# Prompt attention kept feature-major: probabilities divided by their sums ahead of their transposes, mean of squares by one matmul

## Chip, cores and metric

One core of one Trainium2 chip. The time is that of the device for one execution, in microseconds (us), as the median of several runs. The engines are named as in the profile: PE (matrix multiplications and transposes; PEld is its weight load), DVE (elementwise work), ACT (activations and copies), POOL (elementwise work, slower), SP (issues most DMAs). PE writes to PSUM, eight banks of 128 x 512 f32; all other tiles lie in SBUF.

## What is computed

One inference step of a decoder layer for a prompt of 1024 tokens and 8 running sequences ("samples") of 8 tokens each, width 1024, all in float32. What matters here is the middle of the layer, the mixer:

```
z = rms_norm(x) @ w_in + b_in          # q, k, v of attention; four parts of a linear recurrence (HGRN2)
# sliding window attention, 8 heads of 64 in 2 groups, window 128, one sink per head
p = exp(s - m);  den = sum(p) + exp(sink - m);  a = (p / den) @ v
a = rms_norm(a) * attn_out_norm        # mean of squares over all 512 features of a token
mix = concat([a, gated recurrence]) @ w_out
x = x + rms_norm(mix) * norm_mix_post
```

In front of it and behind it stands a gated FFN of width 2816 each (w_gu, w_down), which makes up most of the multiplications.

## The kernel before

**Tiling.** The 1088 tokens are worked in three groups of 320, 384 and 384 (`WIDTH`); group 0 holds 256 prompt tokens and the 64 sample tokens. Attention runs in blocks of 128 prompt tokens, two, three and three of them (`NPB`), so eight in all. Each large product is made of three PE instructions on operands split into a rounded part and a remainder (`mm3`, L260 to L262); `split` (L240, L241) makes the parts, a copy on ACT and a subtraction on DVE. Weights stream in through `raw` tiles, are split, and are used once.

**Order.** The mixer of a group is a Python generator (`mixer`, L1635): it joins the chain of recurrence steps with the chain of attention blocks and yields between pieces of work. `tick()` advances it a little after each half of a streamed product (`stream`, `tick`, L99 to L110), so that the mixer's small PE instructions lie between the large products of `w_in_units`, `w_out_units` and the FFNs; `need` runs the rest of it at once. The program is then put in order at build time from a simulated timeline (`schedule_with_timeline_sim=True`, L1921): on each engine the earliest piece of program whose inputs are ready by that simulation goes first. At run time every engine works through its queue in that order.

**An attention block** (`attn_block`, L1215) works on pairs of heads, `pr` = 0 and 1, in both groups of heads at once. The scores `sc` (L1237) go through a masked maximum on DVE (L1247) and an exponential on ACT (L1255) with the queries as rows; the exponential's sum goes to `mx[:, 1]`, and L1259 makes the sink's exponential. Two yields later PE transposes the probabilities (`pT`, L1269), ACT and DVE copy them to SBUF (L1274), and one yield later the products `pv` (L1283) with the values give the result feature-major: the feature as the row, the query as the column, in `of_`. After the second pair, the sums and the sink are added and inverted for all heads (L1296, L1297), and PE transposes `of_` back to queries as rows (`pvT`, L1301, four instructions); DVE multiplies by the inverted sums as it evicts (L1303).

`finish_attn` (L1199) then normalizes: a square with its sum on ACT (L1202), an inverse root on one column on DVE (L1203 and `rsqrt`, L224 to L229), a multiplication with the root and the gain `aon` (L1205). Three yields later PE transposes the result once more (`oT`, L1211, four instructions), and `put_mix` (L1193) splits it into `MT`, the input of `w_out`: a copy on ACT (L1196), the remainder on DVE (L1197). The samples have an attention of their own (`sample_attn`, L1470), with queries as rows throughout, which ends in the same `finish_attn`. `w_out_units(0)` takes all 320 tokens of group 0 in each product, so it waits for the samples too.

**Buffers.** Small tiles come from `t2` (8 buffers in SBUF) and `ax` (4 PSUM banks), shared by all streams. `mean_root` (L290) is the inverse root for the other norms: one matmul with a constant matrix sums over the rows, and six DVE and two ACT instructions follow.

Of the kernel before, what the change touches and what calls it, by code (L numbers as in the profile page):

```python
# [47 lines left out]
def tile_step(ctx: ExitStack, tc: tile.TileContext, A: dict, O: list):  # L48
# [17 lines left out]
    def axbank(s="ax"):  # L66
        return ps.tile([P, 512], F32, tag="ax", bufs=4, name=uid(s))
# [219 lines left out]
    def tmp2(name, shape=(P, 512)):  # L287
        return pp.tile(list(shape), F32, tag="t2", bufs=8, name=uid(name))

    def mean_root(ss, dst=None):  # L290
        w = ss.shape[-1]
        bank = axbank("rb")
        y = tmp2("rt")[:, :w]
        x = bank[:, :w]
        made = PE.matmul(x, omean, ss, start=True, stop=True)
        t = tmp2("mt")[:, :w]
        V.tensor_scalar(y.bitcast(I32), x.bitcast(I32), -0.5, float(MAGIC), op0=ALU.mult, op1=ALU.add)
        S.activation(t, y, AF.Square)
        V.tensor_tensor(t, x, t, op=ALU.mult)
        V.scalar_tensor_tensor(y, t, -3.0 * RS ** 2, y, op0=ALU.add, op1=ALU.mult)  # L300
        S.activation(t, y, AF.Square)
        V.tensor_tensor(t, x, t, op=ALU.mult)
        q = tmp2("mq")[:, :w]
        V.scalar_tensor_tensor(q, t, -40.0 / 3 * RS ** 6, t, op0=ALU.add, op1=ALU.mult)
        end = V.scalar_tensor_tensor(x if dst is None else dst, q, 80.0 * RS ** 12, y, op0=ALU.add, op1=ALU.mult)
        return made, x, end

    def sum_squares(E, ss, sq, d):
# [770 lines left out]
    def mixing(tp, h):  # L1079
        w_in, w_out = A["w_in"], A["w_out"][0]  # L1080

        def t2(shape=(P, 512)):
            return tmp2("t2", shape)

        aon = tp.tile([P, 512], F32, tag="aon", name="aon")
        nc.sync.dma_start(aon, A["attn_out_norm"][0:1].partition_broadcast(P))
        bhi = tp.tile([P, 512], F32, tag="bhi", name="bhi")
        nc.sync.dma_start(bhi, A["b_in"][0:1, 1792:2304].partition_broadcast(P))

# [103 lines left out]
        def put_mix(n, half, sl, src):  # L1193

            hi, lo = MT[n][0][half], MT[n][1][half]
            S.copy(hi[:, :, sl], src)  # L1196
            V.tensor_tensor(lo[:, :, sl], src, hi[:, :, sl].bitcast(F32), op=ALU.subtract)  # L1197

        def finish_attn(n, o, r, sl):  # L1199

            sm = small()
            S.activation(junk[:r], o[:r], AF.Square, accum_out=sm[:r, 0, 0:1])  # L1202
            V.tensor_scalar(sm[:r, 0, 0:1], sm[:r, 0, 0:1], 1.0 / 512, EPS, op0=ALU.mult, op1=ALU.add)  # L1203
            rsqrt(sm[:r, 1, 0:1], sm[:r, 0, 0:1], (sm[:r, 2, 0:1], sm[:r, 3, 0:1]))
            V.scalar_tensor_tensor(o[:r], o[:r], sm[:r, 1, 0:1], aon[:r], op0=ALU.mult, op1=ALU.mult)  # L1205
            yield
            yield
            yield
            b4 = axbank("oT").rearrange("p (c t) -> p c t", c=4)
            for c in range(4):  # L1210
                PE.transpose(b4[:, c, :r], o[:r, c * P:(c + 1) * P], ident[:r, :r])  # L1211
            put_mix(n, 0, sl, b4[:, :, :r])
            yield

        def attn_block(n, b):  # L1215
# [9 lines left out]
            def of(x, pr):  # L1225
                return x.rearrange("p (g r i) -> p g r i", g=2, r=2)[:, :, pr]
# [4 lines left out]
            for pr in range(2):  # L1231
# [25 lines left out]
                                     scale=0.125, accum_out=mx[:, 1, hd:hd + 1])  # L1257
                V.tensor_tensor(of(sm[:, 2], pr), of(sm[:, 1], pr), of(nsinkb, pr), op=ALU.subtract)
                S.activation(of(sm[:, 2], pr), of(sm[:, 2], pr), AF.Exp)  # L1259
                yield  # L1260
                yield
                pT, tb2 = [], [axbank("pT").rearrange("p (g i s q) -> p g i s q", g=2, i=2, s=2) for _ in range(2)]
# [28 lines left out]
                else:  # L1291
                    S.copy(src, ob[0])
                    V.tensor_tensor(src, ob[1], src, op=ALU.add)
                if pr:
                    yield
            V.tensor_tensor(mx[:, 2], mx[:, 1], sm[:, 2], op=ALU.add)  # L1296
            V.reciprocal(mx[:, 3], mx[:, 2])  # L1297
            yield
            tb = axbank("pvT")
            for m in range(4):  # L1300
                PE.transpose(tb[:, m * P:(m + 1) * P], of_[:, m * P:(m + 1) * P], ident)  # L1301
            o = t2()
            V.tensor_tensor(o.rearrange("p (g m d) -> p m g d", g=2, m=4),  # L1303
                            tb.rearrange("p (m g d) -> p m g d", m=4, g=2),
                            mx[:, 3].rearrange("p (g m) -> p m g", g=2).unsqueeze(3).to_broadcast([P, 4, 2, 64]),
                            op=ALU.mult)
            yield from finish_attn(n, o, P, slice(b * P, (b + 1) * P))

        def intra(n, res):

# [159 lines left out]
        def sample_attn():  # L1470
# [65 lines left out]
            for b in range(8):  # L1536
                for g in range(2):
                    nc.sync.dma_start(
                        o[8 * b:8 * b + 8, 256 * g:256 * g + 256].rearrange("t (m d) -> t m d", m=4),
                        osc[2 * g + b // 4, 32 * (b % 4):32 * (b % 4) + 32].rearrange("(m t) d -> t m d", m=4))  # L1540
            yield
            yield from finish_attn(n, o, NS, slice(256, 320))
# [318 lines left out]
def _laid_out(inputs):  # L1861

    import numpy as np

    a = {k: np.asarray(v) for k, v in inputs.items()}

    def columns(x):
        return x.reshape(-1, P).T

    def feature_major(x):  # L1870
        return x.T.reshape(KC, P, -1).transpose(1, 0, 2).reshape(P, -1)

# [6 lines left out]
    out = {k: a[k] for k in ("cache_k_win", "cache_v_win", "state_hgrn", "b_in", "attn_sinks", "attn_out_norm", "w_out",  # L1879
                             "ffn1_w_down",  # L1880
                             "ffn2_w_down", "norm_ffn1_post", "norm_mix_post", "norm_ffn2_post")}
    out.update(
        x0T=feature_major(np.concatenate([xp[:256], a["x_sample"].reshape(NS, D)])),
        xT=np.stack([feature_major(xp[256:640]), feature_major(xp[640:1024])]),
        x_rest=xp[256:],
        ffn1_w_gu=tiles(a["ffn1_w_gu"][0]), ffn2_w_gu=tiles(a["ffn2_w_gu"][0]), w_in=tiles(w_in[:, paired]),
        w_val=w_in[:, 1792:2304].reshape(4, 2, P, 512).transpose(0, 2, 1, 3).reshape(4, P, 1024),
        norm_ffn1_pre=columns(a["norm_ffn1_pre"]),
        cols=np.concatenate([columns(x) for x in (
            a["norm_ffn1_post"], a["norm_mix_pre"], a["norm_mix_post"], a["norm_ffn2_pre"], a["norm_ffn2_post"],  # L1890
            b[paired], a["hg_lb_logits"], a["hg_out_norm"], a["attn_out_norm"])], axis=1),
        sample_sinks=np.tile(np.repeat(a["attn_sinks"].reshape(2, 4).T, 8, axis=0), (4, 1)),
        cache_kT=a["cache_k_win"][0].reshape(8, P, P).transpose(2, 0, 1).reshape(P, 8 * P))
    return {k: np.ascontiguousarray(v) for k, v in out.items()}
# [30 lines left out]
```

## Time and profile before

| | |
|---|---|
| median of 3 runs | 1935.81 us (1934.51 to 1936.41) |
| the profiled execution | 1934.69 us, span of its instructions 1933.0 us |
| granted PE clock | 0.999 |
| moved by DMA | 375.56 MB, 194 GB/s over the span |
| PE transposes pvT and oT | 32 and 36 instructions, first at 769.9 us, last at 1286.1 us |

Rows of the profile are read as: line, engine, operation, output <- input by the program's names, shape, count, then busy us in all and mean ns of one, then the idle us of the engine just before them and what ended it. Busy time of PE overlaps, since one matmul starts before the one ahead of it has ended. In a timeline the first two columns are the start and the duration in us.

### The profile page before, as it was taken

To read this page: it belongs to the slowest core of one execution; us is meant where nothing else is said; L and a number is where in the kernel's file an instruction comes from. 1 tells how busy PE (TensorE), PEld (TensorE's weight loads), DVE (VectorE), ACT (ScalarE), POOL (GpSimd) and SP (SyncE) were. 2 spreads that over 40 slices of the span, in tenths; PEclk is the share of its full clock that TensorE was granted. 3 is DMA by queue.
4 is the path that set the end of the run, shared out by engine and by line. 5 is a ranking of instruction groups with operands and counts; after the bars stand their busy time and mean duration, and the time that the engine had idled before them with its cause. 6 is when DMAs were issued, how large, how long until landed. Compare 5 with 4: busy or idle time off the path is not lost.

```text
span 1933.0 us, 34860 instructions
## 1 busy us (share of the span) xinstructions
PE 1921.4 (99%) x13555; PEld 1807.3 (93%) x13555; DVE 1429.5 (74%) x2471; ACT 950.6 (49%) x1704; POOL 187.4 (10%) x227
## 2 busy tenths in 40 slices
PE   9999999999999999999999999999999999999998
PEld 9999999999998987788999888989999999999886
DVE  7896789887568666787678757756987787656666
ACT  5553444444455434545445545846544444445452
POOL 0300000000004023120222212000000000000202
PEclk9999999999999999999999999999999999999999
DMA  6643676555767546765434344446555555667974
GB/s 249 209 133 115 233 271 253 199 189 186 241 216 246 178 158 216 282 219 164 124 99 146 102 142 147 156 152 203 190 200 195 189 190 193 210 227 238 311 255 141
DMA packets 175750, 375.56 MB, mean 194 GB/s; under 512 B 16144, under 2 KB 67536, under 8 KB 175568
## 3 DMA queue, kind: packets, MB, share of 16 engines
q1 hardware_dynamic: 169680, 362.84, 55.3%
q10 hardware_dynamic: 5904, 10.49, 1.6%
q8 instruction: 106, 1.74, 0.4%
q14 instruction: 60, 0.49, 0.1%
HBM read 290.86 MB, written 83.39 MB: 194 GB/s over the span
## 4 chain that ended last, share of the span: by engine, by line
PE 94%; DMA 3%; DVE 1%; ACT 1%; issue 1%; POOL 0%; SPq 0%; ACTq 0%; DVEq 0%; POOLq 0%
PE mm L260 29%; PE mm L261 29%; PE mm L262 29%; DMA ar<-act 1%; PE lv L1337 1%; PE sc L1237 1%; PE pv L1283 1%; DMA ar<-fa 1%; PE pT L1269 1%; PE c L260 0%; PE c L262 0%; PE c L261 0%; DMA big<-in_ffn_w_gu_dram 0%; DMA gb<-in_norm_ffn_post_dram 0%; DMA x1N<-big 0%
## 5 line engine op out<-in xcount | busy, mean ns | idle before, releaser
L260 PE MATMUL mm<-h,wsph 128*128 128x320 f32 (+1 forms) x1344 | 427.2, 319 | 0.3 <-DVE big L814 0.3
L261 PE MATMUL mm<-h,wsph 128*128 128x320 f32 (+1 forms) x1344 | 425.8, 317 | 0.1
L262 PE MATMUL mm<-h,wspl 128*128 128x320 f32 (+1 forms) x1344 | 422.7, 316 | 0.0
L241 DVE TENSOR_TENSOR wspl<-raw,wsph 128x1024 fp32r<-128x1024 f32 x208 | 258.8, 1245 | 124.0 <-ACT wsph L240 122.7
L240 ACT CAST wsph<-raw 128x1024 fp32r<-128x1024 f32 x208 | 218.4, 1051 | 253.8 <-PE mm L261 199.3
L261 PEld LDWEIGHTS mm<-h,wsph 128*128 128x128 f32 x1344 | 252.5, 188 | 4.0 <-issue 2.5
L260 PEld LDWEIGHTS mm<-h,wsph 128*128 128x128 f32 x1344 | 252.2, 188 | 4.1 <-issue 2.1
L262 PEld LDWEIGHTS mm<-h,wspl 128*128 128x128 f32 x1344 | 251.9, 188 | 2.0 <-issue 1.6
L240 ACT CAST w<-raw 128x512 fp32r<-128x512 f32 (+1 forms) x208 | 154.2, 748 | 192.9 <-PE mm L261 86.3
L261 PE MATMUL mm<-h,w 128*128 128x384 f32 (+1 forms) x736 | 245.6, 334 | 0.4 <-DVE h L622 0.4
L260 PE MATMUL mm<-h,w 128*128 128x384 f32 (+1 forms) x736 | 245.7, 334 | 0.0
L262 PE MATMUL mm<-h,w 128*128 128x384 f32 (+1 forms) x736 | 239.6, 333 | 0.6 <-POOL w L613 0.5
L241 DVE TENSOR_TENSOR w<-raw,w 128x512 fp32r<-128x512 f32 (+1 forms) x208 | 178.4, 862 | 74.2 <-ACT w L240 73.5
L261 PE MATMUL mm<-w,h 128*128 128x512 f32 x462 | 180.5, 391 | 0.4 <-DVE w L241 0.4
L260 PE MATMUL mm<-w,h 128*128 128x512 f32 x462 | 180.8, 394 | 0.0
L262 PE MATMUL mm<-w,h 128*128 128x512 f32 x462 | 179.8, 391 | 0.0
L261 PE MATMUL mm<-big,w 128*128 128x384 f32 x528 | 176.4, 334 | 0.0
L260 PE MATMUL mm<-big,w 128*128 128x384 f32 x528 | 176.4, 334 | 0.0
L262 PE MATMUL mm<-big,w 128*128 128x384 f32 x528 | 175.9, 334 | 0.0
L261 PEld LDWEIGHTS mm<-h,w 128*128 128x128 f32 x736 | 138.1, 188 | 1.1 <-DVE h L622 0.9
L262 PEld LDWEIGHTS mm<-h,w 128*128 128x128 f32 x736 | 137.6, 188 | 1.1 <-POOL w L613 0.7
L260 PEld LDWEIGHTS mm<-h,w 128*128 128x128 f32 x736 | 138.1, 188 | 0.5 <-ACT h L620 0.2
(370 smaller groups left out, 3363.6 us busy)
## 6 DMA issues: line engine op xcount, KB each, us to landing
raw<-in_ffn_w_gu_dram SPq DMA_DIRECT2D x162, 512.0 KB
raw<-in_ffn_w_down_dram SPq DMA_DIRECT2D x74, 512.0 KB
raw<-in_w_in_dram SPq DMA_DIRECT2D x54, 512.0 KB
ar<-fa SPq DMA_DIRECT2D x70, 384.0 KB
big<-in_ffn_w_down_dram SPq DMA_DIRECT2D x88, 256.0 KB
fb<-big SPq DMA_DIRECT2D x44, 512.0 KB
fa<-big SPq DMA_DIRECT2D x22, 768.0 KB
raw<-fb SPq DMA_DIRECT2D x30, 512.0 KB
```

The source lines that it names most:

```text
L240: made['S'] = S.copy(hi, src).ins
L241: (lo_eng or V).tensor_tensor(lo, src, hi.bitcast(F32), op=ALU.subtract)
L260: PE.matmul(out, a[0], b[0], start=first, stop=False, skip_group_check=resume)
L261: PE.matmul(out, a[0], b[1], start=False, stop=False, skip_group_check=resume)
L262: return PE.matmul(out, a[1], b[0], start=False, stop=last, skip_group_check=resume).ins
L1237: PE.matmul(banks[g][rows(hq), i, cs], zq[rows(g), 2 * pr + i, b * P + 64 * hq:b * P + 64 * hq + 64], kx[rows(g), k0 + cs.start:k0 + cs.st ...
L1269: PE.transpose(tb2[hq][:, g, i, slot], pt[g][rows(hq), c:c + P], ident[rows(hq), rows(hq)])
L1283: PE.matmul(ob[par][rows(g), :, hq], vn[rows(par), b + (blk + hq) // 2, rows(g)], pT[hq][rows(par), g, :, PLACE[hq][blk]], start=alone or ...
L1337: PE.matmul(b5[32 * i:32 * i + 32, b, a], K[:, a, cs], Q[:, a, cs], start=True, stop=True)
```

## The change

In each prompt block the result stays feature-major from `pv` to `MT`. The probabilities are multiplied by the inverted sums of their own pair of heads before they are transposed. The squares of the result are taken feature-major into `dg`; two additions on DVE bring them to 128 columns, and one f32 matmul with a matrix of ones (`ms`) sums over the rows and leaves the mean of squares in each row. The same eight instructions as in `mean_root`, now a helper `newton`, make the inverse root, and one multiplication applies it to all four row blocks. The gain is a scale per row, applied on ACT. The transposes `pvT` and, for prompt blocks, `oT` are gone. Since the feature order of `MT` is now that of the paired heads, the rows of `w_out` and the gains are permuted on the host, and the samples put their result in that order as it is read back. In `finish_attn`, now for the samples alone, the gain is applied by four ACT instructions behind the transposes; the row of gains `aon` and its load are gone.

```
+    def newton(y, x, t, q, dst):
+        V.tensor_scalar(y.bitcast(I32), x.bitcast(I32), -0.5, float(MAGIC), op0=ALU.mult, op1=ALU.add)
+        S.activation(t, y, AF.Square)
+        V.tensor_tensor(t, x, t, op=ALU.mult)
+        V.scalar_tensor_tensor(y, t, -3.0 * RS ** 2, y, op0=ALU.add, op1=ALU.mult)
+        S.activation(t, y, AF.Square)
+        V.tensor_tensor(t, x, t, op=ALU.mult)
+        q = q() if callable(q) else q
+        V.scalar_tensor_tensor(q, t, -40.0 / 3 * RS ** 6, t, op0=ALU.add, op1=ALU.mult)
+        return V.scalar_tensor_tensor(dst, q, 80.0 * RS ** 12, y, op0=ALU.add, op1=ALU.mult)
...
-        aon = tp.tile([P, 512], F32, tag="aon", name="aon")
-        nc.sync.dma_start(aon, A["attn_out_norm"][0:1].partition_broadcast(P))
+        dg = tp.tile([P, 512], F32, tag="dg", name="dg")
...
         def finish_attn(n, o, r, sl):
...
-            V.scalar_tensor_tensor(o[:r], o[:r], sm[:r, 1, 0:1], aon[:r], op0=ALU.mult, op1=ALU.mult)
+            V.tensor_scalar(o[:r], o[:r], sm[:r, 1, 0:1], None, op0=ALU.mult)
...
-            put_mix(n, 0, sl, b4[:, :, :r])
+            t = t2((P, 4, r))
+            for c in range(4):
+                S.activation(t[:, c], b4[:, c, :r], AF.Copy, scale=gain(c))
+            put_mix(n, 0, sl, t)
+            yield
+
+        def finish_block(n, o, sl):
+            o = o.rearrange("p (m q) -> p m q", m=4)
+            y, t, ss, q = [dg[:, i * P:(i + 1) * P] for i in range(4)]
+            V.tensor_tensor(dg[:, :256], dg[:, :256], dg[:, 256:], op=ALU.add)
+            V.scalar_tensor_tensor(ss, y, EPS / P, t, op0=ALU.add, op1=ALU.add)
+            for m in range(4):
+                S.activation(o[:, m], o[:, m], AF.Copy, scale=gain(m))
+            yield
+            yield
+            x = axbank("ms")[:, :P]
+            PE.matmul(x, ones, ss, start=True, stop=True)
+            newton(y, x, t, q, ss)
+            yield
+            yield
+            yield
+            V.tensor_tensor(o, o, ss.unsqueeze(1).to_broadcast([P, 4, P]), op=ALU.mult)
+            put_mix(n, 0, sl, o)
             yield
...
                 S.activation(of(sm[:, 2], pr), of(sm[:, 2], pr), AF.Exp)
+                V.tensor_tensor(of(mx[:, 2], pr), of(mx[:, 1], pr), of(sm[:, 2], pr), op=ALU.add)
+                V.reciprocal(of(mx[:, 3], pr), of(mx[:, 2], pr))
+                for g in range(2):
+                    hd = 4 * g + 2 * pr
+                    p = pt[g][:, 64:448].rearrange("p (i c) -> p i c", i=2)[:, :, cs]
+                    V.tensor_tensor(p, p, mx[:, 3, hd:hd + 2].unsqueeze(2).to_broadcast(list(p.shape)), op=ALU.mult)
                 yield
                 yield
...
-                if pr:
-                    yield
-            V.tensor_tensor(mx[:, 2], mx[:, 1], sm[:, 2], op=ALU.add)
-            V.reciprocal(mx[:, 3], mx[:, 2])
-            yield
-            tb = axbank("pvT")
-            for m in range(4):
-                PE.transpose(tb[:, m * P:(m + 1) * P], of_[:, m * P:(m + 1) * P], ident)
-            o = t2()
-            V.tensor_tensor(o.rearrange("p (g m d) -> p m g d", g=2, m=4),
-                            tb.rearrange("p (m g d) -> p m g d", m=4, g=2),
-                            mx[:, 3].rearrange("p (g m) -> p m g", g=2).unsqueeze(3).to_broadcast([P, 4, 2, 64]),
-                            op=ALU.mult)
-            yield from finish_attn(n, o, P, slice(b * P, (b + 1) * P))
+                S.activation(dg[:, pr * 256:pr * 256 + 256], of_[:, pr * 256:pr * 256 + 256], AF.Square,
+                             scale=512.0 ** -0.5)
+            yield from finish_block(n, of_, slice(b * P, (b + 1) * P))
...
                     nc.sync.dma_start(
-                        o[8 * b:8 * b + 8, 256 * g:256 * g + 256].rearrange("t (m d) -> t m d", m=4),
+                        o[8 * b:8 * b + 8].rearrange("t (m g d) -> t g m d", m=4, g=2)[:, g],
...
+        w_out=np.concatenate([w_out[heads], w_out[512:]])[None],
```

More of the change, by code (lines that the diff above doesn't have):

```diff
@@ L295, in mean_root @@
         made = PE.matmul(x, omean, ss, start=True, stop=True)
[L296 to L305, printed above, removed]
+        end = newton(y, x, tmp2("mt")[:, :w], lambda: tmp2("mq")[:, :w], x if dst is None else dst)
         return made, x, end
@@ L1197, in put_mix, with gain @@
             V.tensor_tensor(lo[:, :, sl], src, hi[:, :, sl].bitcast(F32), op=ALU.subtract)
+        def gain(c):
+            return cols[:, C_AON + c:C_AON + c + 1]
         def finish_attn(n, o, r, sl):
@@ L1878, in _laid_out @@
     paired = np.array(heads + list(range(512, 2816)))
-    out = {k: a[k] for k in ("cache_k_win", "cache_v_win", "state_hgrn", "b_in", "attn_sinks", "attn_out_norm", "w_out",
+    w_out = a["w_out"][0]
+    out = {k: a[k] for k in ("cache_k_win", "cache_v_win", "state_hgrn", "b_in", "attn_sinks",
                              "ffn1_w_down",
@@ L1890, in _laid_out @@
             a["norm_ffn1_post"], a["norm_mix_pre"], a["norm_mix_post"], a["norm_ffn2_pre"], a["norm_ffn2_post"],
[L1891 removed]
+            b[paired], a["hg_lb_logits"], a["hg_out_norm"], a["attn_out_norm"][:, heads])], axis=1),
         sample_sinks=np.tile(np.repeat(a["attn_sinks"].reshape(2, 4).T, 8, axis=0), (4, 1)),
```

## The prediction

> **What bounds the kernel now.** I read the page first: the busy shares, then the chain that ended last.
>
> ```profile
> span 1933.0 us, 34860 instructions
> PE 1921.4 (99%) x13555; PEld 1807.3 (93%) x13555; DVE 1429.5 (74%) x2471; ACT 950.6 (49%) x1704; POOL 187.4 (10%) x227
> ...
> PE 94%; DMA 3%; DVE 1%; ACT 1%; issue 1%; POOL 0%; SPq 0%; ACTq 0%; DVEq 0%; POOLq 0%
> ```
>
> PE is busy for 99% of the span and is 94% of the chain. Next, the windows around the change: the mixers run from about 700 to 1300 us, the second FFN behind them. The columns after the length are the busy us (instructions) of PE, PEld, DVE, ACT and POOL, then the granted clock.
>
> ```profile
> 700.00:1300.00 600.00, 598.47 (x5845) 531.58 (x5845) 435.11 (x920) 315.79 (x654) 115.39 (x152) 1.00 0.50 162
> 1300.00:1900.00 600.00, 600.00 (x3416) 575.10 (x3415) 445.61 (x677) 286.07 (x478) 13.28 (x11) 1.00 0.63 218
> ```
>
> Where the change works, PE is idle for 600 - 598.47 = 1.5 us. So a PE instruction that goes takes its own issue time off the kernel, and work on DVE (435 of 600 us busy) or ACT (316) costs nothing until PE has to wait for it. The first question is then what PE's instructions cost: a group's duration is not its cost, since matmuls overlap. Hence the groups by line on PE, and behind them PE's timeline around one group of four transposes and one of four f32 matmuls.
>
> ```profile
> L1461 PE MATMUL u<-big,t 128*128 128x128 f32 x64 | 8.4, 275 | 0.0
> L1301 PE MATMUL pvT<-ident,t 128*128 128x128 f32 x32 | 5.4, 275 | 0.0
> L1211 PE MATMUL oT<-ident,t 128*128 128x128 f32 (+1 forms) x36 | 5.3, 269 | 0.0
> L1269 PE MATMUL pT<-ident,t 64*128 64x64 f32 x240 | 12.8, 232 | 0.0
> ```
>
> ```profile
> 1031.57 0.33 PE L262 MATMUL mm<-h,wspl 128*128 128x384 f32 x1
> 1031.74 1.05 PE L1461 MATMUL u<-big,t 128*128 128x128 f32 x8
> ...
> 1032.81 0.34 PE L261 MATMUL mm<-h,wsph 128*128 128x384 f32 x1
> ...
> 1112.26 0.31 PE L260 MATMUL mm<-h,wsph 128*128 128x320 f32 x1
> 1112.41 0.60 PE L1211 MATMUL oT<-ident,t 128*128 128x128 f32 x4
> ...
> 1113.00 0.31 PE L262 MATMUL mm<-h,wspl 128*128 128x320 f32 x1
> ```
>
> From the product at 1112.26 to the one at 1113.00, with one product between that is left out, are 0.74 us. Two products take two pitches of 0.15 (1112.26 to 1112.41), so four transposes cost 0.44 us, 0.11 each. Around the f32 matmuls it is 1031.57 to 1032.81, 1.24 us, less two pitches of 0.17: 0.90 us for four matmuls (eight records, an f32 matmul leaves two), 0.225 each.
>
> **The change part by part.**
>
> *PE, prompt blocks.* Eight blocks lose four transposes pvT (x32 above) and four oT (32 of the 36; the samples keep four): 64 x 0.11 = 7.0 us go. Each gains one f32 matmul of 128x128 by 128x128 for the mean of squares: 8 x 0.225 = 1.8 us. Net -5.2 us.
>
> *DVE.* Nothing here is on PE's path as long as DVE keeps up, so the load counts. The prices, of DVE and then of ACT (mean ns behind the busy us):
>
> ```profile
> L1303 DVE TENSOR_TENSOR t<-pvT,sm 128x512 f32<-128x512 f32 x8 | 5.5, 687 | 6.1 <-PE pvT L1301 6.1
> L1205 DVE SCALAR_TENSOR_TENSOR t<-t,sm,aon 128x512 f32<-128x512 f32 x8 | 6.0, 749 | 0.1
> L219 DVE SCALAR_TENSOR_TENSOR sm<-sm 128x1 f32<-128x1 f32 x16 | 3.5, 217 | 0.4
> L503 DVE TENSOR_SCALAR big<-big,sm 128x512 f32<-128x512 f32 x3 | 1.3, 478 | 0.0
> L1293 DVE TENSOR_TENSOR t<-pv,t 128x256 f32<-128x256 f32 x14 | 5.9, 420 | 5.0 <-ACT t L1292 5.0
> L241 DVE TENSOR_TENSOR h<-ar,h 128x384 fp32r<-128x384 f32 x3 | 1.7, 559 | 1.9 <-ACT h L240 1.9
> L1466 DVE SCALAR_TENSOR_TENSOR st<-st,big,u 128x128 f32<-128x128 f32 x28 | 7.8, 337 | 0.3 <-PE u L1461 0.2
> L1197 DVE TENSOR_TENSOR h<-t,h 128x512 fp32r<-128x512 f32 x8 | 6.3, 782 | 0.0
> ...
> L1202 ACT ACTIVATE junk<-t 128x512 bf16<-128x512 f32 x8 | 5.0, 630 | 3.2 <-DVE t L1303 3.2
> L1292 ACT COPY t<-pv 128x256 f32<-128x256 f32 x14 | 5.1, 368 | 10.2 <-PE pv L1283 10.2
> L1400 ACT ACTIVATE t<-av 128x128 f32<-128x128 f32 x32 | 8.3, 269 | 1.6 <-PE av L1457 1.5
> ```
>
> A block loses L1303, L1205 and seven instructions on one column (L1203 and the rsqrt), at most 0.22 each by L219: 0.69 + 0.75 + 1.5 = 2.9 us. It gains four multiplications of the probabilities, 128x384 (the L241 row of that size): 2.24; the sum of halves on 256 columns (L1293): 0.42; seven instructions on 128 columns, one for the sum and six of newton (L1466, an upper end): 2.36; the last multiplication (as L1197, two SBUF operands): 0.78; a second pair of denominator and reciprocal: at most 0.43. That is 6.2, net +3.3 us a block, +26 us in all. 435 + 26 = 461 of 600 us, 77%. The cover: behind 1300 us DVE is busy for 445.61 of 600 us and PE for all 600. If that cover failed, weight remainders (L241) would come late and PE would wait with them.
>
> *ACT.* A block gains two squares of 256 columns, four gains and two squares of 128 columns, 2 x 0.37 + 6 x 0.27 = 2.4 us, and loses L1202, 0.63 (its accumulator read stays uncounted): at most +1.7, 14 us on 316. Hidden likewise.
>
> *The wait that is added.* The transposes pT now stand behind a sum, a reciprocal and two multiplications on DVE, 2 x 0.22 + 2 x 0.56 = 1.6 us later than before. Queued behind pT on PE are the products of the streaming weights. First, a tight one, and the last of 16 pairs, from the end of the sink's exponential to pT:
>
> ```profile
> 727.80 0.19 ACT L1259 ACTIVATE sm<-sm 128x4 f32<-128x4 f32 x1
> 732.09 0.46 PE L1269 MATMUL pT<-ident,t 64*128 64x64 f32 x8
> ...
> 1254.32 0.34 PE L1269 MATMUL pT<-ident,t 64*128 64x64 f32 x3
> 1254.32 0.19 ACT L1259 ACTIVATE sm<-sm 128x4 f32<-128x4 f32 x1
> ...
> 1265.62 0.19 ACT L1259 ACTIVATE sm<-sm 128x4 f32<-128x4 f32 x1
> ...
> 1267.23 0.34 PE L1269 MATMUL pT<-ident,t 64*128 64x64 f32 x4
> ```
>
> The slack is 4.1 us in the first, none in the second, 1.4 in the last; I found five of the 16 pairs below 1.6 us. Bounds: if PE has nothing to slip in, those five cost about 0 to 1.6 us each, at most 5 us together; if the plan, made at build time from a simulated timeline, puts products ahead of pT, nothing. I take nothing, since the nearest row, L1269, shows 0.0 us of idle PE ahead of pT today although pT there follows exponentials that just ended. Below nothing there is little: PE's whole idle time is 1.5 us.
>
> *The samples.* They keep their transposes, and four ACT scalings are put between oT and the copy to MT. At this place PE does wait, since w_out of group 0 needs all its tokens:
>
> ```profile
> 941.57 0.51 PE L1211 MATMUL oT<-ident,t 64*128 64x64 f32 x4
> ...
> 942.45 0.36 ACT L1196 CAST h<-oT 128x256 fp32r<-128x256 f32 x1
> ...
> 943.72 0.42 DVE L1197 TENSOR_TENSOR h<-oT,h 128x256 fp32r<-128x256 f32 x1
> ...
> 944.39 0.71 PE L260 MATMUL mm<-h,wsph 128*128 128x320 f32 x3
> ```
>
> The products at 944.39 follow the remainder that ends at 944.14, and what could fill the gap (the next mixer's first matmuls) is used up. Four scalings at L1400's 0.27 are 1.08 us; the gain no longer multiplied on DVE gives back 0.75 - 0.48 = 0.27 (L1205, L503). I take +0.8, between 0 (hidden) and 1.1.
>
> *Counted at nothing:* one load less at the start of mixing (aon, 0.25 MB against the 375.56 MB moved in all); dg takes its room; w_out's rows and the gains are permuted on the host; the samples' 16 reads change only where they land. One bank (ms) is asked for where two were (pvT, oT), and one t2 tile less a block, so no wait for buffers is added; if newton held its bank long, pT or sc would wait, bounded by the pair waits above. The step count of a block stays twelve, so the streams keep their pace.
>
> **Sum:** -7.0 + 1.8 + 0.8 = -4.4 us. The profiled execution took 1934.69 us, its span 1933.0 plus 1.7 around it; that gives 1930.3. It lies 1.1 below the median of 1935.81, from which the sum gives 1931.4. The runs of before spread over 1.9 us, and I predict 1931.2. A difference of 0.2%, 3.9 us, is about what a measurement of this kernel can tell from no change; the forecast stands only just beyond it.
>
> **The rivals.**
>
> *1. Late probabilities eat the gain.* For it: the five tight pairs. Against it: L1269's 0.0 idle. With half of their 5 us it is -4.4 + 2.5 = -1.9 us, 1933.9: no difference to tell.
>
> *2. DVE waits for POOL, and pT with it: slower.* The same remainder, with its first operand in PSUM and in SBUF (ns, min/median/max), and POOL's largest group:
>
> ```profile
> L1197 DVE TENSOR_TENSOR h<-oT,h x9: 418/684/692, 783.1 to 1287.2; 128x512 fp32r<-128x512 f32 x8, 128x256 fp32r<-128x256 f32 x1
> L1197 DVE TENSOR_TENSOR h<-t,h x9: 427/684/1456, 797.1 to 1256.6; 128x512 fp32r<-128x512 f32 x8, 128x256 fp32r<-128x256 f32 x1
> ...
> L1388 POOL TENSOR_TENSOR big<-big,big 128x768 f32<-128x768 f32 x12 | 25.0, 2082 | 102.6 <-PE lv L1337 100.9 <-PE l L1377 1.5
> ```
>
> With two SBUF operands it once took 0.77 us longer. All four multiplications of a block are of that kind and POOL is busy 115 of 600 us. If each of the 32 were held up by 0.77, pT would be 1.6 + 1.5 = 3.1 us later, past the slack of some nine pairs by about 1.5 on the mean: +13.5, so -4.4 + 13.5 = +9.1 us, 1944.9. It decides for slower once the 16 pairs cost PE 8.3 us, 0.52 each. Against it: the median of 684 says that most such instructions aren't held up. The Trainium skill, "SBUF — State Buffer", section "Who interferes with whom", states that a DVE instruction with two SBUF inputs contends with a GpSimd instruction that reads SBUF; that speaks against this change, and the maximum of 1456 agrees. If POOL were reading at every one of the 32, that rule would give this rival's time; it reads in at most 19% of these 600 us.
>
> *3. Transposes cost their duration.* If each removed one gave back its 272 ns (L1301's and L1211's means) and each f32 matmul took two records of 275, it would be -64 x 0.272 + 16 x 0.275 + 0.8 = -12.2 us, 1923.6. Against it: four in 0.60 us in the timeline. The Trainium skill, "TensorE: Matmul & The Clock Gate", section "Part 4: PE-mode transpose", gives about 275 ns for one in a kernel's context; the rows agree as to the duration, not as to the cost.
>
> *4. PE's freed time isn't the bound,* and another queue sets the end: 0 us, 1935.8. Against it: PE's 94% of the chain and DMA's 3%.
>
> **How the numbers follow.** Forecast, with -3.9 to -8 us: 0.50. Rival 1: 0.27. Rival 2: 0.14. Rival 3: 0.04. Rival 4: 0.05. Faster by over 0.2%: 0.50 + 0.04 = 0.54; within: 0.27 + 0.05 = 0.32; slower: 0.14. Below, the range takes in the forecast with PE's idle time and the seams' small waits gone, -9: 1926.8. Above, it takes in rivals 1 and 4 and the start of rival 2: 1938.0. Left out are rival 3 and most of rival 2, under 0.2.
>
> **What would show it.** Right: pvT gone, oT x4, ms x16, PE busy some 5 us less, PE idle in the mixers below 3 us, DVE there at 460 us. Wrong: idle PE ahead of pT (rivals 1, 2), its releaser DVE; the multiplications well above 0.56 us (rival 2); PE busy down by 12 us or more (rival 3); fewer busy us on PE but the same span (rival 4).

## The result and the profile after

| | before | after |
|---|---|---|
| median | 1935.81 us | 1941.46 us (1938.99 to 1943.03, 7 runs) |
| ratio to before, 95% interval | 1 | 1.0032 (1.0020 to 1.0044) |
| the profiled execution, its span | 1934.69, 1933.0 us | 1938.99, 1937.3 us |

Slower by 5.65 us, where 4.6 less were forecast, and outside the range of 1926.8 to 1938.0. The page of the changed kernel, busy us of each engine and the chain that ended last:

```profile
span 1937.3 us, 34849 instructions
...
PE 1918.5 (99%) x13507; PEld 1804.6 (93%) x13507; DVE 1448.8 (75%) x2519; ACT 961.9 (50%) x1756; POOL 188.1 (10%) x227
...
PE 90%; DMA 3%; DVE 3%; ACT 2%; issue 1%; POOL 0%; SPq 0%; DVEq 0%; POOLq 0%; ACTq 0%
```

PE is busy for 2.9 us less than before (1921.4) and has 48 records fewer (64 transposes gone, 16 records of ms come), as the change says. But the span is 4.3 longer, so PE's idle time went from 11.6 to 18.8 us, and PE's part of the chain from 94% to 90%. The windows of the changed kernel say where (columns as in the prediction):

```profile
700.00:1300.00 600.00, 591.31 (x5783) 525.47 (x5783) 456.25 (x967) 326.46 (x702) 117.50 (x152) 1.00 0.51 161
...
1200.00:1300.00 100.00, 94.69 (x745) 87.06 (x744) 70.33 (x174) 67.80 (x149) 1.75 (x12) 0.98 0.47 150
...
1270.00:1275.00 5.00, 2.69 (x41) 2.15 (x42) 3.11 (x6) 3.61 (x6) 0.00 (x0) 0.81 0.22 65
1275.00:1280.00 5.00, 5.00 (x31) 5.00 (x32) 2.10 (x6) 2.85 (x7) 0.00 (x0) 0.85 0.63 208
```

Of 600 us PE is idle for 8.7 (before: 1.5), 5.3 of them between 1200 and 1300. And the granted clock falls to 0.81 as the mean of 5 us. What PE waited for in the changed kernel (us in all, times, longest):

```profile
PE mm L260 <- ACT h L1197: 2.7, 1, 2.7
PE pT L1302 <- DVE t L1292: 2.4, 1, 2.4
PE pv L1316 <- DVE t L1307: 1.3, 2, 1.1
...
PE mm L260 <- ACT sg L718: 0.9, 1, 0.9
```

Two places carry most of it. **The samples' end**, at 946.78: ACT's timeline of the changed kernel, behind the transposes oT at 941.83.

```profile
942.71 0.92 ACT L1218 ACTIVATE t<-oT,cols 128x64 f32<-128x64 f32 x4
943.65 1.28 ACT L1191 ACT_TABLE_LOAD   x1
944.95 1.48 ACT L1191 ACTIVATE big<-big 128x1536 f32<-128x1536 f32 x1
946.34 0.39 ACT L1197 CAST h<-t 128x256 fp32r<-128x256 f32 x1
```

In the kernel before, ACT had this order:

```profile
942.45 0.36 ACT L1196 CAST h<-oT 128x256 fp32r<-128x256 f32 x1
942.83 1.28 ACT L1190 ACT_TABLE_LOAD   x1
944.13 1.49 ACT L1190 ACTIVATE big<-big 128x1536 f32<-128x1536 f32 x1
```

The four scalings take 0.92 us in all (1.08 were costed). But the copy to `MT`, which stood directly behind oT before, now stands behind a table load and an activation of 1.48 us that belong to the recurrence. The copy comes 3.9 us later, not one.

**The end of the last block**, PE's timeline of the changed kernel:

```profile
1259.22 0.71 PE L1302 MATMUL pT<-ident,t 64*128 64x64 f32 x16
...
1264.90 0.89 PE L1316 MATMUL pv<-t,vn 64*64 64x128 f32 x24
1265.61 0.83 PE L1264 MATMUL sc<-kx,big 64*64 64x192 f32 x16
...
1268.38 0.31 PE L262 MATMUL mm<-h,wspl 128*128 128x320 f32 x1
1271.12 1.05 PE L1302 MATMUL pT<-ident,t 64*128 64x64 f32 x16 [2.43 <-DVE t L1292]
1273.23 1.56 PE L1316 MATMUL pv<-t,vn 64*64 64x128 f32 x24 [1.06 <-DVE t L1307]
1274.72 0.63 PE L260 MATMUL mm<-h,wsph 128*128 128x320 f32 x1
...
1276.48 0.32 PE L260 MATMUL mm<-h,wsph 128*128 128x320 f32 x1
```

And the same stretch before, from the last scores to the first pT of that pair:

```profile
1261.44 0.83 PE L1237 MATMUL sc<-kx,big 64*64 64x192 f32 x16
1262.20 0.41 PE L261 MATMUL mm<-h,wsph 128*128 128x320 f32 x1
...
1266.99 0.31 PE L260 MATMUL mm<-h,wsph 128*128 128x320 f32 x1
1267.23 0.34 PE L1269 MATMUL pT<-ident,t 64*128 64x64 f32 x4
```

Before, there were 33 products between the last scores and pT (1262.20 to 1267.23); now there are 14, which end at about 1268.7, and then PE stands until the last multiplication of the probabilities is done. From the end of these scores to pT pass 4.7 us now (1266.44 to 1271.12); 33 products at a pitch of 0.147 would fill 4.9, so by this estimate the old number of products would have covered the longer chain too.

Behind the two waits the clock falls: in this trace the granted clock is 0.50 from 1273.1 to 1276.5 us, 3.41 us long, and 1.00 on both sides. The same 24 products take 1.56 us in place of 0.89 there, and six large products from 1274.72 to 1276.48 take 1.76 where six pitches of 0.147 are 0.88: some 1.6 us more for the lower clock. (The 16 transposes, 1.05 us in place of 0.71, still lie at full clock; what stretches them is not shown.) So the account of the profiled execution is: busy -2.9, which is +1.6 of clock and, by difference, -4.5 of work, and +7.2 of idle time, +4.3 in all. The profiled execution is the fastest of the seven. The six other runs of after had a mean clock of 0.995 to 0.997 against 0.999 in the profiled one, and took 1941.29 to 1943.03 us; before had 0.998 to 1.000 in all runs beside the experiments. The medians are 5.65 us apart, and the account explains 4.3 of them; that the other 1.35 are more time at low clock fits these means, but no trace of a slower run shows it.

### The profile page after: what moved, and what is told of

Read it like the earlier page. It is cut to its first block, busy times and chain, and to the rows that moved or that the text cites. A ratio compares the mean times of both kernels' runs of the same rounds, so it can differ in the third digit from the quotient of the medians.

```text
span 1937.3 us, 34849 instructions
## 1 busy us (share of the span) xinstructions
PE 1918.5 (99%) x13507; PEld 1804.6 (93%) x13507; DVE 1448.8 (75%) x2519; ACT 961.9 (50%) x1756; POOL 188.1 (10%) x227
## 4 chain that ended last, share of the span: by engine, by line
PE 90%; DMA 3%; DVE 3%; ACT 2%; issue 1%; POOL 0%; SPq 0%; DVEq 0%; POOLq 0%; ACTq 0%
PE mm L260 28%; PE mm L261 28%; PE mm L262 28%; DMA ar<-act 1%; PE lv L1359 1%; DMA ar<-fa 1%; PE pv L1316 1%; PE sc L1264 1%; PE c L262 0%; PE c L260 0%; PE c L261 0%; DMA big<-in_ffn_w_gu_dram 0%; DVE wspl L241 0%; ACT t L1282 0%; DMA x1N<-big 0%
```

## The experiments

The expectations name the theories as they stood then. **A:** the loss is the two waits just shown, the samples' scalings and the division ahead of pT; each can be taken away by itself, and the savings add up. **B:** the larger load and the new plan slow the mixers all along, at no single place. **C:** ACT and DVE are full in some stretches, and PE waits for the work added there. **D:** the order is finely set against one graph; whatever moves the pieces of a mixer against the streamed products, even less work, costs several us. All times stand beside before on the same chip (1935.1 to 1935.9 us). The kernels e2, e3, i1 and i2 leave out a part of the computation, so only their times are of use. The last two columns come from one profiled execution of each kernel, which can lie some us from the median (e2 1940.07 and i1 1951.68 us are the farthest).

| kernel | median us | ratio, 95% interval | PE idle, 700 to 1300 us | last product of the samples (spv) at |
|---|---|---|---|---|
| before | 1935.81 | 1 | 1.5 | 927.4 |
| after | 1941.46 | 1.0032 (1.0020 to 1.0044) | 8.7 | 927.7 |
| e1 samples put back | 1941.41 | 1.0027 (1.0017 to 1.0037) | 8.5 | 928.1 |
| e2 no division | 1945.32 | 1.0042 (1.0029 to 1.0055) | 8.9 | 926.3 |
| e3 both | 1940.96 | 1.0026 (1.0017 to 1.0035) | 6.8 | 926.4 |
| e4 after, rates 7 to 10% up | 1962.98 | 1.0137 (1.0122 to 1.0153) | 23.6 | 936.8 |
| f1 before, rates 2% up | 1950.36 | 1.0076 (1.0063 to 1.0088) | 9.9 | 938.1 |
| f2 before, rates 2% down | 1947.74 | 1.0054 (1.0041 to 1.0066) | 7.3 | 940.1 |
| f3 after, rates 2% down | 1954.95 | 1.0103 (1.0086 to 1.0120) | 14.4 | 938.1 |
| f4 after, gains on DVE | 1939.12 | 1.0016 (1.0007 to 1.0025) | 6.1 | 928.2 |
| g1 f4, last mixer sooner | 1943.93 | 1.0042 (1.0029 to 1.0056) | 9.3 | 928.2 |
| g2 f4 and e1 | 1938.66 | 1.0016 (1.0007 to 1.0025) | 7.4 | 929.5 |
| g3 g1 and e1 | 1944.49 | 1.0044 (1.0032 to 1.0057) | 8.7 | 926.8 |
| g4 after, rates 2% up | 1954.72 | 1.0101 (1.0087 to 1.0114) | 17.3 | 934.3 |
| h1 f4, last mixer later | 1941.11 | 1.0026 (1.0017 to 1.0035) | 7.1 | 928.5 |
| h2 f4, later still | 1939.73 | 1.0019 (1.0011 to 1.0028) | 6.0 | 928.4 |
| h3 before and the division | 1950.52 | 1.0076 (1.0064 to 1.0088) | 13.9 | 935.9 |
| h4 h1 and e1 | 1940.65 | 1.0023 (1.0015 to 1.0032) | 9.2 | 931.1 |
| i1 before without oT | 1946.05 | 1.0054 (1.0040 to 1.0068) | 12.2 | 934.9 |
| i2 before without oT, pvT | 1929.80 | 0.9973 (0.9963 to 0.9983) | 1.9 | 926.9 |

### The two waits taken away (e1 to e3)

e1 gives the samples their old end: the row of gains, loaded into `dg`, multiplied ahead of oT, and the split straight from PSUM.

```
-            V.tensor_scalar(o[:r], o[:r], sm[:r, 1, 0:1], None, op0=ALU.mult)
+            V.scalar_tensor_tensor(o[:r], o[:r], sm[:r, 1, 0:1], dg[:r], op0=ALU.mult, op1=ALU.mult)
...
-            for c in range(4):
-                S.activation(t[:, c], b4[:, c, :r], AF.Copy, scale=gain(c))
-            put_mix(n, 0, sl, t)
+            put_mix(n, 0, sl, b4[:, :, :r])
```

> The samples alone are put back: their gain is again one multiplication with a row of gains ahead of the transposes, and the copy to MT reads PSUM. Theory A (two seams): PE's wait of 2.7 us for this copy at 946.8 us goes, and with it about 2.7 us: 1938.8 us against 1941.5 of the change, the wait before pT near 1271 us stays. Theory B (the larger load on DVE and ACT and the new plan slow the mixers all along): no difference beyond 1 us, 1941.5.

e2 drops the multiplications of the probabilities (L1289 to L1292), e3 does both.

```
-                for g in range(2):
-                    hd = 4 * g + 2 * pr
-                    p = pt[g][:, 64:448].rearrange("p (i c) -> p i c", i=2)[:, :, cs]
-                    V.tensor_tensor(p, p, mx[:, 3, hd:hd + 2].unsqueeze(2).to_broadcast(list(p.shape)), op=ALU.mult)
```

> The multiplications of the probabilities by their inverted sums are left out, so the prompt attention's result is undivided; all else as in the change. Theory A: the wait of PE before pT (2.4 us), the one before pv behind it (1.1 us) and the lower clock that follows them (0.81 and 0.85 over ten us, 1.7 us) go, about 5 us: 1936.5 us; the wait of 2.7 us for the samples stays. Theory B: DVE loses 16.5 us of work, the gain is spread over all blocks and may come to the whole 10.8 us to the forecast, 1931.

> Both at once: no division, samples with the row of gains. Theory A: the two gains add up, 1941.5 - 2.7 - 5.2 = 1933.6 us, and PE's idle time between 700 and 1300 us falls to below 3 us. Theory B: as without the division alone, within 1 us.

Each edit takes away the wait that it aims at, and none gains clearly: e1 and e3 lie within 0.5 us of after, e2 3.9 above it. In e1 the samples' 2.7 us are gone, but two waits of 0.73 and 0.79 us stand behind that place (at 957 and 966) and two of 0.87 and 0.72 ahead of it (at 808 and 822), and the clock of the window, 1.00 in after, is 0.98:

```profile
900.00:1000.00 100.00, 98.28 (x1298) 88.69 (x1297) 67.71 (x122) 48.01 (x87) 26.24 (x28) 0.98 0.37 109
```

The waits on PE in e2, and behind it in e3:

```profile
PE tr L515 <- ACT t L1321: 4.2, 1, 4.2
PE mm L260 <- ACT h L1197: 2.7, 1, 2.7
```

```profile
PE tr L515 <- DVE big L505: 4.3, 1, 4.3
```

In e2 the wait ahead of pT is gone, and one of 4.2 us stands at other transposes (L515, the next norm) some 55 us earlier. In e3 both known waits are gone and one of 4.3 us is there. PE's idle time between 1200 and 1300 us is 5.2 to 5.6 us in all three. A falls: the waits are not two causes that add up. B had e1 right (no difference), but not e2, for which it allowed 1931.

### The pace of the mixers (e4, f1 to f3, g4)

One line, the rates at which steps of the three mixers are drawn:

```
-    RM = [0.88, 1.08, 1.24]
+    RM = [0.96, 1.16, 1.36]
```

for e4 on the changed kernel; 0.90, 1.10, 1.26 for f1 (before) and g4 (after); 0.86, 1.06, 1.22 for f2 (before) and f3 (after).

> The change as it is, but the mixers are stepped faster (0.96, 1.16 and 1.36 steps per tick instead of 0.88, 1.08 and 1.24), so that they end with products still to come. Theory A: both seams are covered by products, 1933 to 1937 us, no wait over 1 us before pT or for the samples' copy. Theory B: the load is the same or denser, 1941 us or more.

> The kernel before, nothing of the change in it, but the mixers' steps are drawn 2% sooner (rates 0.90, 1.10, 1.26 in place of 0.88, 1.08, 1.24), so that each piece of a mixer lies a few products away from where it lay. Theory D (the order is set finely against one graph; any shift of the mixers' pieces against the streamed products puts exponentials ahead of weight parts that PE needs next): slower than before by 3 to 8 us, with PE idle of 3 us and more between 900 and 1300 us, at a place that is not that of the changed kernel. Theory C (ACT and DVE are full in some stretches, and it is the work that the change adds there that PE waits for): no such work is added here, so within 2 us of 1935.8.

> The kernel before with the mixers' steps drawn 2% later (rates 0.86, 1.06, 1.22). Theory D: slower by 3 to 8 us, or, if the shift to later is the kind one, within 2 us; both this and the run with 2% sooner within 2 us would speak against it. Theory C: within 2 us of 1935.8.

> The changed kernel with the mixers' steps drawn 2% later (0.86, 1.06, 1.22). Nothing is added or removed. Theory D: the time moves by 3 us or more in either direction, and the waits of 2.7 and 2.4 us lie elsewhere; if the places happen to suit, 1930 to 1934, which is the sum of the prediction. Theory C: the same work in the same stretches, 1940 to 1943.

> The changed kernel with all three rates 2% higher (0.90, 1.10, 1.26), the third pair of before and after at equal rates: at the rates of the kernel before the change costs 5.7 us, at 2% less 7.2 (1955.0 against 1947.7); before at 2% more is 1950.4. If the change has a cost of its own beside the tuning (more work and a longer chain in each block, Theory C), it is slower here too, by 3 to 9 us: 1953 to 1959. If all is a matter of where pieces fall (Theory D), the difference is as likely to be of the other sign, anywhere from 1940 to 1960, and an answer below 1948 would say so.

The kernel before, with not an instruction changed, loses 14.6 us at 2% more and 11.9 at 2% less: far more than the change costs, and more than the 3 to 8 that D had expected. C alone can't give that. PE's largest wait in f1, and PE's timeline of f1 there:

```profile
PE oT L1211 <- DVE t L1205: 7.2, 1, 7.2
```

```profile
938.05 0.31 PE L1529 MATMUL spv<-vnew,t 8*32 8x64 f32 x8
...
952.18 0.70 PE L1211 MATMUL oT<-ident,t 64*128 64x64 f32 x4 [7.19 <-DVE t L1205]
```

The samples' last product comes at 938.05, where it was at 927.42 before (their three earlier rounds are late too, by 5 to 11 us), and about 14 us pass from it to oT in both kernels. In before the first 8 of them are the way of the result through DRAM: the square on it (L1202, at 935.24) waits for the DMA that reads it back. Before has products for these 14 us; in f1 the last one starts at 944.65. And in f1 the square stands behind the recurrence's activation that held up the samples' copy in the changed kernel:

```profile
947.25 1.48 ACT L1190 ACTIVATE big<-big 128x1536 f32<-128x1536 f32 x1
948.64 0.61 ACT L1202 ACTIVATE junk<-t 64x512 bf16<-64x512 f32 x1
```

This one activation parts the traces. In twelve of them (after, e2, e4, f1, f3, f4, g1, g4, h1, h2, h3, i1) it, or the DVE instruction that waits for it (L1191 in the kernel before), lies ahead of some step of the samples' normalization or of their copy to `MT`, and PE waits there for 2.7 us, or for 5.8 to 7.2 ahead of oT. In the other eight, before and i2 among them, it lies behind the copy, and PE has no such wait.

The table's last column goes with the times: where the samples end at 934 us or later, 1946 to 1963 us; where they end by 931, 1930 to 1945. But the step between the two is only 0.7 us wide (i1 and e2), and one wait isn't the reason for all of it. In f2 the samples end at 940.1 and PE doesn't wait for them at all between 900 and 1000 us; 5.5 of its 7.3 us of idle time lie between 800 and 900:

```profile
PE spT L1517 <- ACT t L1512: 3.6, 1, 3.6
PE sc L1237 <- ACT t L1448: 1.9, 1, 1.9
```

What makes the samples' rounds late I haven't traced.

At equal rates, after is slower than before each time: by 7.2 us (f3 against f2), 5.7 (at the rates as they are) and 4.4 (g4 against f1). So the change isn't only unlucky at one setting, and g4 came where C had put it (1953 to 1959), if inside D's wider range too; but three settings, each with its own waits, do not separate a cost of its own from the order's.

### Gains on DVE, and a search from there (f4, g1 to g3, h1, h2, h4)

```
-            for m in range(4):
-                S.activation(o[:, m], o[:, m], AF.Copy, scale=gain(m))
...
-            V.tensor_tensor(o, o, ss.unsqueeze(1).to_broadcast([P, 4, P]), op=ALU.mult)
+            for m in range(4):
+                V.scalar_tensor_tensor(o[:, m], o[:, m], gain(m), ss, op0=ALU.mult, op1=ALU.mult)
```

> The changed kernel, but the four scalings by the gain on ACT go, and the last multiplication on DVE takes the gain as its scalar (four instructions of 128 columns, about 0.3 us each, in place of one of 0.78): ACT has 1.1 us a block less, DVE 0.4 more. The results are the same. Theory C, with ACT as the full engine: PE's idle between 1200 and 1300 us falls from 5.3 to 3 us or less, and the time to 1936 to 1939. Theory D: the time moves by any amount, and PE's idle does not follow ACT's load.

g1, h1 and h2 add only the last mixer's rate (1.26, 1.22 and 1.20 for 1.24); g2 adds e1's edit; g3 and h4 add e1's edit to g1 and h1.

> The changed kernel with the gains in the last multiplication on DVE (1939.1 us by itself), and the last mixer's rate alone raised from 1.24 to 1.26, so that its last block comes some 3 to 4 us sooner against the products. If the waits at the end of the last block (1.8 and 1.1 us, with the low clock behind them) are there because that block comes too late against the weights (Theory D, one rate out of tune), they go: 1934 to 1937, and PE's idle between 1200 and 1300 us below 1 us; the samples' 2.7 us stay. If they are there because ACT and DVE have too much work in those 100 us (Theory C), the waits only move within them: 1938 to 1941.

> The changed kernel with the gains in the last multiplication on DVE, and the samples as they were (their gains as a row, multiplied ahead of the transposes, the split straight from PSUM). Theory C: with less on ACT the stretch behind the samples (950 to 980 us), which took the 2.7 us back when the samples were put back by themselves, has room, so 1939.1 less 2.7 and the low clock behind it: 1935 to 1937. Theory D: the order behind the samples is made anew, and waits of 1 to 3 us in all show at other places: 1938 to 1941.

> All three together: gains on DVE, samples as they were, and the last mixer's rate at 1.26. If both places are a matter of where pieces lie against the products, and each edit settles its own, PE's idle between 700 and 1300 us falls under 3 us and the time to 1930 to 1934, the sum of the prediction and below the kernel before. If a stall that is taken away at one place comes up at the next, 1936 to 1941.

> The changed kernel with the gains on DVE (1939.1 us by itself) and the last mixer's rate lowered from 1.24 to 1.22, where 1.26 gave 1943.9 and a wait of 5.5 us ahead of the last pT. In all of them the last scores lie close behind the products of a unit whose banks come free only behind the copy of pT on ACT, so that PE has nothing to do while the chain from sc to pT runs (about 5.5 us). Theory D: a later mixer puts more products between those scores and pT, so the waits of 1.8 and 1.1 us and the low clock go: 1934 to 1937. Theory C: 1938 to 1941.

> As before this, with the last mixer's rate at 1.20. Theory D: 1934 to 1938, if the kind place is wide; if the rate is finely set, the loss is back at another place, as with the kernel before at 2% less: 1942 to 1950. Theory C: 1938 to 1941 once more.

> Gains on DVE, samples as they were, last mixer's rate at 1.22. If the waits in the last mixer go with the lower rate, and those of 0.7 to 1.3 us behind the samples stay as in the run at 1.24 (1938.7): 1933 to 1936. If not: 1937 to 1941.

f4 gains 2.3 us on after (their intervals overlap), the wait ahead of pT is down from 2.4 to 1.8 us, and PE's idle time in its window from 5.3 to 3.1; it speaks for C a little:

```profile
1200.00:1300.00 100.00, 96.86 (x755) 89.70 (x754) 71.33 (x184) 65.02 (x143) 1.75 (x12) 0.97 0.46 148
```

The rate of the last mixer does not do what D expected of the single place: sooner (g1) makes the wait 5.5 us, not less, and later takes it down to 0.5 (h1) or away (h2), but the samples' 2.7 stays and 1.3 to 2.3 us come up at the last block's copy to `MT`, near 1293 us. g2 came as D had put it, g3 above both forecasts. ACT's timeline of g1, where PE stands from about 1268.1 to 1273.64:

```profile
1272.30 0.19 ACT L1285 ACTIVATE sm<-sm 128x4 f32<-128x4 f32 x1
1275.12 0.58 ACT L1306 COPY t<-pT 128x512 f32<-128x512 f32 x1 [2.63 <-PE pT L1301]
1275.61 0.76 ACT L718 COPY sg<-mm 128x320 f32<-128x320 f32 x2
```

ACT is idle for 2.63 us, and then copies pT's result ahead of the two banks of the FFN (L718), while DVE has no weight remainder left to make (its last one ended at 1268.9). That the next products waited for these banks is likely but argued: they stand behind pT and pv in PE's order anyway, and the profile names only pT's wait. None of the seven comes below before; the nearest, g2 and f4, are 0.16% above it (0.07 to 0.25).

### One half, and less than before (h3, i1, i2)

h3 is the kernel before with the division alone: sums, reciprocal and multiplications as in the change, and the eviction of pvT made a copy. i1 leaves out the prompt blocks' oT, i2 oT and pvT.

```
+            if r == P:
+                put_mix(n, 0, sl, o.rearrange("p (c t) -> p c t", c=4))
+                yield
+                return
...
-            tb = axbank("pvT")
-            for m in range(4):
-                PE.transpose(tb[:, m * P:(m + 1) * P], of_[:, m * P:(m + 1) * P], ident)
+            tb = of_
```

(the second part in i2 only)

> The kernel before, and of the change only the division: each pair's sums, reciprocal and two multiplications on DVE ahead of its transposes; pvT, its eviction (now a copy), the old normalization and oT stay. PE does the same work as before. If the division's longer chain is the change's own cost, this is slower than before by 3 to 8 us, with DVE as the releaser of pT: 1939 to 1944. If the cost lies in the normalization kept feature-major (its latency, its ACT work), this is within 2 us of 1935.4.

> The kernel before, with the transposes oT of the prompt blocks left out (the split reads the block's result as it lies; the samples keep theirs): 32 PE instructions fewer, nothing added, the rates untouched. By the prediction's arithmetic 32 x 0.11 = 3.5 us go: 1931 to 1934. Theory D (any change of the graph makes the order anew, and the rates suit only the old graph): waits of 2 to 6 us in all at new places, 1935 to 1945.

> As before this, and the transposes pvT left out as well (DVE's multiplication reads the result in SBUF as it lies): 64 PE instructions and two PSUM banks a block fewer, nothing added, and the chain of each block is shorter. By the prediction's arithmetic -7.0 us: 1927 to 1931. Theory D: 1932 to 1945, with waits at new places. If it comes in at 1927 to 1931, the change's loss is a cost of what it adds (Theory C).

h3 loses 14.7 us, though e2, the change without the division, isn't faster than after: the two halves lose 14.7 and 9.5, together 5.7. They can't be added, so the loss can't be shared out between them; and h3's longest wait, 6.1 us, isn't at a division, but ahead of the samples' oT as in f1. And i1, with 32 PE instructions less than before and nothing more, loses 11 us (10.95 by the medians). PE's largest wait in i1, and the window's PE busy time:

```profile
PE oT L1215 <- issue: 6.1, 1, 6.1
```

```profile
900.00:1000.00 100.00, 93.00 (x1258) 82.76 (x1257) 65.41 (x121) 43.84 (x77) 21.46 (x27) 0.97 0.35 105
```

It is f1's place again, the samples' last product 7.5 us late (934.88), with 7 us of idle PE in this window; on DVE the recurrence's L1191, at 949.36, stands between the steps of the samples' inverse root (L1203 at 944.43, L229 at 950.47). i2 doesn't slip, and there the arithmetic of the prediction holds. Page and window of i2:

```profile
PE 1916.2 (99%) x13491; PEld 1801.0 (93%) x13491; DVE 1429.4 (74%) x2471; ACT 950.2 (49%) x1706; POOL 187.3 (10%) x227
```

```profile
700.00:1300.00 600.00, 598.12 (x5805) 529.63 (x5805) 438.40 (x922) 317.60 (x657) 116.10 (x152) 1.00 0.50 163
```

PE is busy for 5.2 us less than before, idle for 1.9 of the 600 us, and the time is 5.3 less: freed PE time is worth its full length where the order stays free of waits. D is shown for a part of what it says: less work can cost 11 us. But not every change of the graph costs, as i2 shows. Its time lies in the range that was to speak for C; that doesn't follow, since i1 adds nothing either and loses. What stays open is the rest. After adds to i2 the eight matmuls ms, the division and the work on DVE and ACT; against before it is 5.65 us slower where i2 is 5.3 faster, 11.0 apart, of which the matmuls are 1.8 by the prediction's price. Whether the other 9 are the price of longer chains and fuller queues (C, for which f4's 2.3 us and the three equal rates speak) or of an order that fell badly (D), the runs don't tell; a search over all three rates for the changed kernel wasn't made.

## Why the prediction was off, by its steps

**PE, prompt blocks (-5.2): the mechanism right, the size a little large.** i2 measures the 64 transposes alone: -5.3 us by the medians (-7.2 to -3.3 by the interval), where -7.0 was put, which lies just inside the interval; so about 0.08 us each by the medians, where 0.11 was put. The whole change took some 4.5 us of work off PE, by the account above.

**DVE and ACT hidden: sizes right, the conclusion failed.** DVE has 456.25 us in the 600 (461 foretold), ACT 326.46 (at most 330). The multiplications were costed at 0.56 us, and this row of the changed kernel (form, count, busy, mean ns, idle before) gives 556 ns:

```profile
L1292 DVE TENSOR_TENSOR t<-t,sm 128x384 f32<-128x384 f32 x28 | 14.4, 556 | 0.4
```

What failed is "costs nothing until PE has to wait for it", judged from a mean over 600 us. PE waited with DVE at 70 and ACT at 68 of 100 us; at the samples' copy it was the order of ACT's queue that held PE up.

**The added wait at nothing: failed.** That the bound of 5 us is near what came is luck: it was five waits of up to 1.6 us, and what came is one pair with 2.4 and 1.1 us of waiting, and 1.6 of low clock, for which the sum had no term. The row that made me choose the low end (L1269 with 0.0 idle) belonged to the order of before, which put 33 products ahead of that pT; the new order puts 14.

**The samples (+0.8, between 0 and 1.1): mis-sized.** The wait is 2.7 us, outside the bounds, since I had added the scalings to an order that stayed; the order put 2.8 us of another stream between them and the copy.

**"The step count of a block stays twelve, so the streams keep their pace": the step that failed first.** The samples do keep their pace in the changed kernel (927.7 us against 927.4), but the sum went on from there as if the order on each engine stayed too. It is made anew from a simulated timeline for every graph: the copy to `MT` went behind the recurrence's activation, and 14 products stood where 33 had stood. i1 and f1 show what a new order can do: 11 to 15 us, from edits that add nothing. No rival held this. The slower case was given to one mechanism, and the range ended 3.5 us below the time.

**The rivals.** Rival 1 named the place (pT behind DVE) but not its size. Rival 2's did not show: the multiplications (ns, min/median/max, in the changed kernel) are all near their median, none with 0.77 us of hold-up:

```profile
L1292 DVE TENSOR_TENSOR t<-t,sm x32: 418/551/619, 729.0 to 1270.9; 128x384 f32<-128x384 f32 x28, 128x256 f32<-128x256 f32 x4
```

So the sentence of the Trainium skill that I weighed there ("SBUF — State Buffer", "Who interferes with whom") may hold, but these multiplications show no price for it. Rival 3 is ruled out by i2 (-5.3, not the 17 that 64 x 0.272 gives), and so is rival 4. Of the signs named, idle PE ahead of pT with DVE as its releaser came true, with PE idle in the mixers 8.7 us where under 3 was the sign of success.

## What to carry to other kernels

Where a build-time plan orders every engine's queue, price an edit twice: by the work that it takes from the bound engine, and by the plan that it makes anew, whose spread is measured by nudging one free parameter of the kernel before (here 2% of a rate, 12 to 15 us, against a saving of 5). A small saving is only to be forecast together with a new tuning, and two versions are best compared at several settings each, not at the one that suits the older.

Averages of busy time over a stage don't show whether added work is hidden: look at the few places where the bound engine has little left to do (here the samples' end and the last block), count the instructions between producer and consumer there, and see what stands ahead in the queue.

## What the runs showed of the hardware

An idle PE costs more than its idle time. In the changed kernel 3.5 us of waiting in two pieces between 1268.7 and 1273.2 were followed by 3.41 us at a granted clock of 0.50, which cost 1.6 us more. In the other traces too, where the clock falls ahead of the kernel's end, it falls to 0.50, for 3.41, 6.83 or 10.24 us at a time. In f1 and f2, whose instructions are those of before, PE is busy for 5.1 and 7.8 us longer than in before, with 10.2 and 13.7 us at this clock; before has none of it ahead of its last 5 us. The length of a wait alone doesn't tell whether the clock falls: the same 2.7 us ahead of the samples' products left it at 1.00 in after, e2 and g1, and were followed by 3.41 us at 0.50 in f4, h1, h2 and f3. The Trainium skill, "TensorE: Matmul & The Clock Gate", "Part 1: The HAM clock gate (the "warmup" mystery)", has the clock halve after an idle window of about 3.4 us; the traces agree as to the half, but 2.7 us of idle PE were enough in four of them. Of the kernels with more than 5 us of PE idle in the mixers all but h4 had a mean clock below 0.999 in most of their runs (after 0.995 to 0.999, e4 0.992 to 0.993); the two with under 2 us, before and i2, had 0.998 and above in all of theirs.
